# Expert slots of the lowest ranks cut from 256 to 242–254 rows, with a partial second block in a mixture-of-experts kernel

## The chip, the cores and the metric

The kernel runs on one core of a Trainium2 chip. The metric is the device time of one execution in microseconds (us); lower is better.

## What is computed

A two-block sequence model over 2048 tokens of width 1024. The first block is a retention and pooling mixer, a mixture of experts and a gated embedding; the second is latent attention beside a state-space model. The change lies in the mixture of experts:

```python
logits = xt @ router_w + router_b                    # 2048 tokens, 32 experts
top_vals, top_idx = lax.top_k(logits, 4)             # each token goes to 4 experts
gates = jax.nn.softmax(top_vals, axis=-1)
...                                                  # rows sorted by expert
gu = lax.ragged_dot(xs, w_gu, group_sizes) + b_gu    # 1024 -> 2048
gate = jnp.minimum(gu[:, ::2], 7.0)
up = jnp.clip(gu[:, 1::2], -7.0, 7.0)
act = (up + 1.0) * (gate * jax.nn.sigmoid(1.702 * gate))
y = lax.ragged_dot(act, w_down, group_sizes) + b_down   # 1024 -> 1024
out = out.at[tok].add(y * gates)                     # added back to each token's row
```

## The kernel before

**Slots.** The 32 experts are sorted on the chip by how many rows they got, and slot j takes the expert of rank j. A slot has a fixed number of rows, `CAPS[j]` (line 49): 312 for the first down to 260 for the 19th, then 256 for the last thirteen (ranks 19 to 31). An expert with fewer rows is filled up with entries of a padding row; what exceeds a slot would be done in an overflow loop of 128-row blocks, which runs zero times with these inputs, before and after.

**One slot.** `start` loads the slot's entries (`ent`: token numbers and gates) by SP, and `gather` lets POOL fetch the token rows by two indirect DMAs of 128 rows (L866, tile `rows`). `turn` transposes a block of 128 rows on PE and splits it into a high and a low part, `xTh` and `xTl`, 128 partitions by n columns, n being the slot's rows. All products are made of three (`mm3`, L142 to L144: high by high, high by low, low by high).

`gate_up` holds a 128x128 block of weights still and moves the n columns of `xTh`/`xTl` past it: 8 column groups x 2 x 8 x 3 = 384 products a slot, n columns each. `swiglu` makes `aTh`/`aTl` of the result. For a slot of 256 rows `down_rows` holds 128 columns of `aTh`/`aTl` still and moves 512 columns of weights: 2 halves h of the output width x 4 pieces x 2 row blocks b x 2 x 3 = 96 products. At the end of each half `done` adds the bias (DVE, L1081), multiplies by the gate (ACT, L1082) and issues on POOL an indirect DMA (L1083) that adds the 128 rows of `yrow`, 2 KB each, to the token rows of `x_h` in DRAM: two scatters, b = 0 and b = 1, behind each half.

**Weights.** A slot's weights come in 24 pieces of 512 KB (16 for `gate_up`, 8 for `down_rows`), one SP DMA each into `raw` (3 buffers); ACT makes `whi` (L135, L160) and DVE `wlo` (L136, L161), 3 buffers each, in the order in which the pieces are used. So a piece's load can begin only when the split three pieces earlier is done.

**Rows above 256** of larger slots go together: four slots share one gather, and after the last of them one small scatter for each slot and half (L1043, tile `rest`) adds `CAPS[j] - 256` rows. The group of ranks 2 to 5 has, in the order of issue, 40, 32, 32 and 24 rows; ranks 0 and 1 have 56 and 48.

**Order of the work.** `S.later(n, f)` queues an action n pieces ahead: the next slot's `start` one piece after the slot before began, its four `turn`s from eight pieces on. State-space work of the second block is interleaved with the slots by the same queue.

Of the kernel before, what the change touches and what calls it, by code (L numbers as in the profile page):

```python
# [15 lines left out]
F32 = mybir.dt.float32  # L16
# [4 lines left out]
OP = mybir.AluOpType  # L21
# [24 lines left out]

CAPS = [312, 304, 296, 288, 288, 280, 280, 280, 280, 272, 272, 272, 272, 264, 264, 264] + [260] * 3 + [256] * 13
NOV = 96  # L50
LE = T + 128
TR = T + 512
# [7 lines left out]
def _const_table():  # L60
    cols = []

    def put(name, a):
        a = np.asarray(a, np.float64)
        if a.ndim == 1:
            a = np.broadcast_to(a, (128, a.shape[0]))
        off = sum(c.shape[1] for c in cols)
        _CST[name] = (off, a.shape[1])
        cols.append(np.ascontiguousarray(a).astype(np.float32))
# [19 lines left out]
    col[:32, 1] = 31 - np.arange(32)  # L89
    col[:32, 2] = CAPS  # L90
    put("ecol", col)
# [41 lines left out]
def split(S, hi, lo, src):  # L133

    S.nc.scalar.activation(hi, src, AF.Copy)  # L135
    S.nc.vector.tensor_tensor(lo, src, hi.bitcast(F32), op=OP.subtract)  # L136


def mm3(S, ps, a, b, start, stop):

    nc = S.nc
    nc.tensor.matmul(ps, a[0], b[0], start=start, stop=False)  # L142
    nc.tensor.matmul(ps, a[0], b[1], start=False, stop=False)  # L143
    nc.tensor.matmul(ps, a[1], b[0], start=False, stop=stop)  # L144


def piece(S, src, shape, g=None):

    nc = S.nc
    raw = S.wp.tile([128, 1024], F32, name="raw", bufs=S.wbufs[0])  # L150
    hi = S.wp.tile([128, 1024], F32R, name="whi", bufs=S.wbufs[1])
    lo = S.wp.tile([128, 1024], F32R, name="wlo", bufs=S.wbufs[1])
    n = shape[0] * shape[1]
    r, h, w = [x[:, :n].rearrange("p (a b) -> p a b", a=shape[0]) for x in (raw, hi, lo)]
    nc.sync.dma_start(r, src)
    if g is None:
        split(S, hi[:, :n], lo[:, :n], raw[:, :n])
    else:
        for k in range(shape[0]):
            nc.scalar.activation(h[:, k, :], r[:, k, :], AF.Copy, scale=g[:, k:k + 1])  # L160
            nc.vector.scalar_tensor_tensor(w[:, k, :], r[:, k, :], g[:, k:k + 1], h[:, k, :].bitcast(F32),  # L161
                                           op0=OP.mult, op1=OP.subtract)
    return h, w
# [72 lines left out]
def transposes(S, dst, src, n):  # L236

    for i in range(n):
        S.nc.tensor.transpose(dst[:, i, :], src[:, i * 128:(i + 1) * 128], S.ident)  # L239
# [603 lines left out]
def shared():  # L843

    out = [[]]
    for j, n in enumerate(CAPS):
        if n > 256:
            if sum(CAPS[i] - 256 for i in out[-1]) + n - 256 > 128:
                out.append([])
# [30 lines left out]
def expert(S, j):  # L880
    return S.nc.sync.value_load(S.erow[0:1, j:j + 1], min_val=0, max_val=NE - 1)


def start(S, j):
    s = S.slots[j] = Slot()
    s.j, s.n = j, CAPS[j]
    s.e = expert(S, j)
    fetch(S, s, S.X["list"][ds(s.e * LE, len(blocks(s.n)) * 128)])
    s.sh = None
    for js in shared():  # L890
        if j == js[0]:
            g = S.sh = Slot()
            g.slots, g.at, g.n = js, {}, 0
            g.ent = S.xp.tile([128, 2, 2], I32, name="ent", bufs=5)
            for i in js:
                m = CAPS[i] - 256
                e = s.e if i == j else expert(S, i)
                S.nc.sync.dma_start(g.ent[g.n:g.n + m, 0], S.X["list"][ds(e * LE + 256, m)])
                g.at[i] = slice(g.n, g.n + m)
                g.n += m  # L900
            gather(S, g, 1, g.n)
        if j in js:
            s.sh, s.at = S.sh, S.sh.at[j]
            s.rest = S.xp.tile([s.n - 256, 2], I32, name="rest", bufs=12)
            S.nc.sync.dma_start(s.rest, S.X["list"][ds(s.e * LE + 256, s.n - 256)])


def phase_c(S):
    nc, A, X = S.nc, S.A, S.X
    wg = A["expert_w_gate_up"][0]  # L910
    wd = A["expert_w_down"][0]
    with ExitStack() as es:
# [33 lines left out]
        def turn(s, b, q):  # L946
            o = b * 128
            ps = S.ps.tile([128, 4, 128], F32, name="tp", bufs=2)
            transposes(S, ps, s.rows[b][:, q * 512:(q + 1) * 512], 4)
            split(S, s.xT[0][:, q * 4:q * 4 + 4, o:o + 128], s.xT[1][:, q * 4:q * 4 + 4, o:o + 128], ps)  # L950

        def turn_shared(g, q):
            n = g.n
# [7 lines left out]
        def turns(s, j):  # L961

            prepare(s, j)
            for i in range(4):
                turn(s, i // 2, i % 2)
                yield
            if s.sh:
                if j == s.sh.slots[0]:
                    for q in range(2):
                        turn_shared(s.sh, q)  # L970
                        yield
                split(S, s.xT[0][:, :, 256:], s.xT[1][:, :, 256:], s.sh.xT[:, :, s.at])
# [14 lines left out]
        def gate_up(s, e, first=()):  # L987
            w = wg[ds(e, 1)].rearrange("o (k p) f -> p (o k) f", p=128)
            s.aT = (p.tile([128, 8, s.n], F32R, name="aTh", bufs=1), p.tile([128, 8, s.n], F32R, name="aTl", bufs=1))
            ready = list(first)  # L990
            for f in range(8):
                acc = [S.ps.tile([128, 512], F32, name="acc", bufs=4) for _ in range(2)]
                for kh in range(2):
                    h, lw = ready.pop(0) if ready else weights(w[:, kh * 4:kh * 4 + 4, f * 256:(f + 1) * 256], True)
                    for g in range(2):
                        for k in range(4):
                            kk = kh * 4 + k
                            mm3(S, acc[g][:, :s.n], (h[:, k, g, :], lw[:, k, g, :]),
                                (s.xT[0][:, kk, :], s.xT[1][:, kk, :]), kk == 0, kk == 7)
                    if kh == 1:  # L1000
                        swiglu(s, f, acc)
                    S.pump()
# [68 lines left out]
        def down_rows(s, e):  # L1071

            w = wd[ds(e, 1)].rearrange("o (k p) f -> p (o k) f", p=128)
            bias = p.tile([128, D], F32, name="bd", tag="br", bufs=1)
            bsrc = A["expert_b_down"][0][ds(e, 1)]
            nc.sync.dma_start(bias, bsrc.broadcast_to([128, D]))
            adds = []

            def done(h, b, acc):
                y = p.tile([128, 512], F32, name="yrow", bufs=3)  # L1080
                nc.vector.tensor_add(y, acc, bias[:, h * 512:(h + 1) * 512])  # L1081
                nc.scalar.mul(y, y, s.ent[:, b, 1:2].bitcast(F32))  # L1082
                add = nc.gpsimd.indirect_dma_start(  # L1083
                    out=X["h1", h], out_offset=bass.IndirectOffsetOnAxis(ap=s.ent[:, b, 0:1], axis=0),
                    in_=y, in_offset=None, compute_op=OP.add)
                for a in adds:
                    S.tc.declare_no_dep(add.ins, a.ins, reason="an expert has no token twice")
                adds.append(add)

            for h in range(2):  # L1090
                acc = [S.ps.tile([128, 512], F32, name="acc", bufs=4) for _ in range(2)]
                for kp in range(4):
                    wh, wl = piece(S, w[:, kp * 2:kp * 2 + 2, h * 512:(h + 1) * 512], (2, 512))
                    for b in range(2):
                        for k in range(2):
                            kk = kp * 2 + k
                            mm3(S, acc[b], [x[:, kk, b * 128:(b + 1) * 128] for x in s.aT], (wh[:, k, :], wl[:, k, :]),
                                kk == 0, kk == 7)
                        if kp == 3:
                            done(h, b, acc[b])  # L1100
                    S.pump()
# [5 lines left out]
        slots = S.slots  # L1107
# [7 lines left out]
        with S.tc.For_i(0, n, 1) as i:  # L1115
            s = Slot()
# [24 lines left out]
        for j in range(NE):  # L1141
            if j + 1 < NE:
                S.later(1, lambda j=j: start(S, j + 1))
                S.later(8, lambda j=j: S.steps(2, turns(slots[j + 1], j + 1)))
            if j == 1:
                S.later(2, s5)
            gate_up(slots[j], slots[j].e, ready if j == 0 else ())
            (down_rows if slots[j].n == 256 else down)(slots[j], slots[j].e)
        S.drain()


# [1083 lines left out]
```

## Time and profile before

| | |
|---|---|
| time, three runs | 4979.05, 4980.39 and 4987.18 us, median 4980.39 us |
| profiled execution | 4985.11 us: a span of 4983.3 us and 1.8 us around it |
| PE busy in the span | 4882.0 us (98%) |
| the slots of 256 rows | about 2444 to 3352 us of the span, some 70 us each |
| mean granted clock of TensorE | 0.993 of full speed |

A time counts the whole execution; the span runs from the first to the last instruction of the profiled one, and all points of time below are counted from its start.

### The profile page before, as it was taken

What the parts mean: (1) busy time and instruction counts of PE and PEld (TensorE: products, weight loads), DVE (VectorE), ACT (ScalarE), POOL (GpSimd) and SP (SyncE); (2) the same over time, 40 slices, a digit from 0 to 9 for tenths busy, and PEclk for the clock granted to TensorE, in tenths of its full rate; (3) what the DMA queues carried; (4) which work ended last, traced back from release to release, by engine and by line L of the source; (5) the groups of instructions that cost most, each with busy time, mean ns of one, the idle gap of its engine ahead of it and who ended that gap; (6) DMA issues with size and microseconds to landing.
All of it is one profiled execution on the core that took longest, in us unless ns stands there. A gap on an engine that the chain in (4) does not pass through costs nothing.

```text
span 4983.3 us, 85621 instructions
## 1 busy us (share of the span) xinstructions
PE 4882.0 (98%) x31503; PEld 4420.4 (89%) x31503; DVE 3414.1 (69%) x7271; ACT 2588.7 (52%) x4530; POOL 901.7 (18%) x910
## 2 busy tenths in 40 slices
PE   9999999899999999999999999999999999999999
PEld 7888788799999999999998999987888888888877
DVE  5666565486666676776777777666666577788686
ACT  4333344455555555555555555545555466666653
POOL 2212234011121103011211111113332300000011
PEclk9999999899999999999999999999999999999999
DMA  5332365566666667676677767766554533222243
GB/s 175 97 95 86 126 234 174 165 188 189 189 202 191 209 184 216 187 222 201 207 223 225 226 212 225 215 210 193 178 175 154 164 112 93 86 71 66 76 151 102
DMA packets 620263, 834.10 MB, mean 167 GB/s; under 512 B 76116, under 2 KB 451716, under 8 KB 619808
## 3 DMA queue, kind: packets, MB, share of 16 engines
q1 hardware_dynamic: 554976, 648.34, 40.7%
q0 software_dynamic: 64864, 180.24, 13.1%
q8 instruction: 250, 4.10, 0.3%
q14 instruction: 173, 1.42, 0.1%
HBM read 685.42 MB, written 143.02 MB: 166 GB/s over the span
## 4 chain that ended last, share of the span: by engine, by line
PE 50%; DVE 5%; DMA 2%; ACT 1%; issue 1%; SPq 0%; POOL 0%; DVEq 0%; ACTq 0%; POOLq 0%
PE acc L142 12%; PE acc L143 12%; PE acc L144 12%; PE tp L239 2%; PE tp L1914 1%; PE oc L142 1%; PE oc L143 1%; PE oc L144 1%; DVE pl L136 1%; DVE mx L1969 1%; PE sc L142 1%; PE sc L143 1%; PE sc L1967 1%; PE sc L144 1%; PE sc L1968 1%
## 5 line engine op out<-in xcount | busy, mean ns | idle before, releaser
L136 DVE TENSOR_TENSOR wlo<-raw,whi 128x1024 fp32r<-128x1024 f32 x810 | 991.3, 1224 | 620.9 <-ACT whi L135 609.9
L135 ACT ACTIVATE whi<-raw 128x1024 fp32r<-128x1024 f32 x810 | 901.0, 1113 | 884.0 <-PE acc L143 440.1
L142 PE MATMUL acc<-xTh,whi 128*128 128x256 f32 (+8 forms) x4096 | 1188.0, 291 | 0.8 <-ACT whi L135 0.8
L144 PE MATMUL acc<-xTh,wlo 128*128 128x256 f32 (+8 forms) x4096 | 1172.5, 288 | 2.1 <-DVE wlo L136 2.0
L143 PE MATMUL acc<-xTl,whi 128*128 128x256 f32 (+8 forms) x4096 | 1174.0, 287 | 0.0
L142 PEld LDWEIGHTS acc<-xTh,whi 128*128 128x128 f32 x4096 | 773.8, 189 | 4.2 <-issue 2.3
L143 PEld LDWEIGHTS acc<-xTl,whi 128*128 128x128 f32 x4096 | 774.6, 189 | 1.0 <-issue 0.5
L144 PEld LDWEIGHTS acc<-xTh,wlo 128*128 128x128 f32 x4096 | 770.4, 189 | 3.3 <-DVE wlo L136 3.1
L143 PE MATMUL acc<-wlo,hTh 128*128 128x512 f32 (+1 forms) x1728 | 679.9, 394 | 0.8 <-DVE wlo L161 0.8
L142 PE MATMUL acc<-whi,hTh 128*128 128x512 f32 (+1 forms) x1728 | 674.6, 398 | 5.0 <-ACT hTh L135 4.3
L144 PE MATMUL acc<-whi,hTl 128*128 128x512 f32 (+1 forms) x1728 | 677.3, 395 | 0.0
L142 PEld LDWEIGHTS acc<-whi,hTh 128*128 128x128 f32 x1728 | 324.6, 189 | 73.1 <-ACT hTh L135 6.0
L143 PEld LDWEIGHTS acc<-wlo,hTh 128*128 128x128 f32 x1728 | 325.9, 189 | 68.0 <-DVE wlo L161 2.0
L144 PEld LDWEIGHTS acc<-whi,hTl 128*128 128x128 f32 x1728 | 325.5, 188 | 67.8 <-DVE hTl L136 0.7
L143 PE MATMUL acc<-aTl,whi 128*128 128x280 f32 (+7 forms) x1216 | 350.4, 291 | 0.2
L142 PE MATMUL acc<-aTh,whi 128*128 128x280 f32 (+7 forms) x1216 | 350.4, 295 | 0.0
L144 PE MATMUL acc<-aTh,wlo 128*128 128x280 f32 (+7 forms) x1216 | 348.7, 291 | 0.0
L142 PEld LDWEIGHTS acc<-aTh,whi 128*128 128x128 f32 x1216 | 226.8, 188 | 6.1 <-ACT whi L135 4.1
L143 PEld LDWEIGHTS acc<-aTl,whi 128*128 128x128 f32 x1216 | 229.2, 189 | 0.7 <-DVE aTl L136 0.7
L144 PEld LDWEIGHTS acc<-aTh,wlo 128*128 128x128 f32 x1216 | 227.6, 188 | 0.0
L1969 DVE TENSOR_REDUCE mx<-sc 128x1 f32<-128x512 f32 x256 | 174.8, 686 | 71.8 <-PE sc L1968 70.2
L866 POOL DMA_INDIRECT rows<-x_xm,row x68 | 81.2, 1194 | 758.3 <-PE acc L144 290.4
(618 smaller groups left out, 9726.0 us busy)
## 6 DMA issues: line engine op xcount, KB each, us to landing
raw<-expert_w_gate_up SPq DMA_DIRECT2D x512, 512.0 KB
raw<-expert_w_down SPq DMA_DIRECT2D x256, 512.0 KB
raw<-w_in SPq DMA_DIRECT2D x128, 512.0 KB
raw<-w_out SPq DMA_DIRECT2D x32, 512.0 KB
raw<-ple_gate_w SPq DMA_DIRECT2D x32, 512.0 KB
ag<-x_ag SPq DMA_DIRECT2D x16, 768.0 KB
x<-x SPq DMA_DIRECT2D x16, 512.0 KB
x_mixT<-mixst POOLq DMA_DIRECT2D x32, 256.0 KB, 4.0
```

Source lines behind the costliest of these rows:

```text
L135: S.nc.scalar.activation(hi, src, AF.Copy)
L136: S.nc.vector.tensor_tensor(lo, src, hi.bitcast(F32), op=OP.subtract)
L142: nc.tensor.matmul(ps, a[0], b[0], start=start, stop=False)
L143: nc.tensor.matmul(ps, a[0], b[1], start=False, stop=False)
L144: nc.tensor.matmul(ps, a[1], b[0], start=False, stop=stop)
L239: S.nc.tensor.transpose(dst[:, i, :], src[:, i * 128:(i + 1) * 128], S.ident)
L866: nc.gpsimd.indirect_dma_start(out=r[:n], out_offset=None, in_=X["xm"], in_offset=bass.IndirectOffsetOnAxis(ap=s.row[:n, b:b + 1], axis=0))
L1914: nc.tensor.transpose(ps[:, kk, t, :], P[t][kt // 4][:, (kt % 4) * 128:(kt % 4 + 1) * 128], S.ident)
L1967: nc.tensor.matmul(Sc[c], qh[:, tr], krT[:, cs], start=False, stop=False)
L1968: nc.tensor.matmul(Sc[c], ql[:, tr], krT[:, cs], start=False, stop=True)
L1969: nc.vector.tensor_reduce(mx[:, c:c + 1], Sc[c], axis=AX.X, op=OP.max)
```

## The change

The last eleven of the thirteen slots of 256 rows get 254, 254, 252, 250, 250, 248, 248, 246, 244, 242 and 242 rows. In all 86 rows are left out. `turn` splits only the first n − 128 columns of the second block; `gate_up` moves n columns; in `down_rows` the second block holds n − 128 columns of `aTh`/`aTl` still, and its bias, gate and scatter take n − 128 rows. The gathers still take 128 rows.

```diff
-CAPS = [312, ..., 264, 264, 264] + [260] * 3 + [256] * 13
+CAPS = [312, ..., 264, 264, 264] + [260] * 3 + [256, 256, 254, 254, 252, 250, 250, 248, 248, 246, 244, 242, 242]
...
             transposes(S, ps, s.rows[b][:, q * 512:(q + 1) * 512], 4)
-            split(S, s.xT[0][:, q * 4:q * 4 + 4, o:o + 128], s.xT[1][:, q * 4:q * 4 + 4, o:o + 128], ps)
+            m = min(s.n - o, 128)
+            split(S, s.xT[0][:, q * 4:q * 4 + 4, o:o + m], s.xT[1][:, q * 4:q * 4 + 4, o:o + m], ps[:, :, :m])
...
             def done(h, b, acc):
+                m = min(s.n - b * 128, 128)
                 y = p.tile([128, 512], F32, name="yrow", bufs=3)
-                nc.vector.tensor_add(y, acc, bias[:, h * 512:(h + 1) * 512])
-                nc.scalar.mul(y, y, s.ent[:, b, 1:2].bitcast(F32))
+                nc.vector.tensor_add(y[:m], acc[:m], bias[:m, h * 512:(h + 1) * 512])
+                nc.scalar.mul(y[:m], y[:m], s.ent[:m, b, 1:2].bitcast(F32))
                 add = nc.gpsimd.indirect_dma_start(
-                    out=X["h1", h], out_offset=bass.IndirectOffsetOnAxis(ap=s.ent[:, b, 0:1], axis=0),
-                    in_=y, in_offset=None, compute_op=OP.add)
+                    out=X["h1", h], out_offset=bass.IndirectOffsetOnAxis(ap=s.ent[:m, b, 0:1], axis=0),
+                    in_=y[:m], in_offset=None, compute_op=OP.add)
...
                         for k in range(2):
                             kk = kp * 2 + k
-                            mm3(S, acc[b], [x[:, kk, b * 128:(b + 1) * 128] for x in s.aT], (wh[:, k, :], wl[:, k, :]),
+                            mm3(S, acc[b][:min(s.n - b * 128, 128)],
+                                [x[:, kk, b * 128:min(s.n, (b + 1) * 128)] for x in s.aT], (wh[:, k, :], wl[:, k, :]),
                                 kk == 0, kk == 7)
...
-            (down_rows if slots[j].n == 256 else down)(slots[j], slots[j].e)
+            (down_rows if slots[j].n <= 256 else down)(slots[j], slots[j].e)
```

On PE, where `gate_up` of the first slot of 250 rows ends and its `down_rows` begins, the order before is this (the shape is that of the result):

```order
L143 MATMUL acc<-xTl,whi 128x256
L144 MATMUL acc<-xTh,wlo 128x256
L142 MATMUL acc<-whi,aTh 128x512
L143 MATMUL acc<-wlo,aTh 128x512
L144 MATMUL acc<-whi,aTl 128x512
L142 MATMUL acc<-whi,aTh 128x512
L143 MATMUL acc<-wlo,aTh 128x512
L144 MATMUL acc<-whi,aTl 128x512
L142 MATMUL acc<-whi,aTh 128x512
L143 MATMUL acc<-wlo,aTh 128x512
L144 MATMUL acc<-whi,aTl 128x512
```

and of the change this:

```order
L143 MATMUL acc<-xTl,whi 128x250
L144 MATMUL acc<-xTh,wlo 128x250
L142 MATMUL acc<-whi,aTh 128x512
L143 MATMUL acc<-wlo,aTh 128x512
L144 MATMUL acc<-whi,aTl 128x512
L142 MATMUL acc<-whi,aTh 128x512
L143 MATMUL acc<-wlo,aTh 128x512
L144 MATMUL acc<-whi,aTl 128x512
L142 MATMUL acc<-whi,aTh 122x512
L143 MATMUL acc<-wlo,aTh 122x512
L144 MATMUL acc<-whi,aTl 122x512
```

No product has moved or gone: those of `gate_up` are 6 columns narrower, and those of the second row block give 122 rows instead of 128. On DVE, around the ends of the two halves of the same `down_rows` (`yrow` is the block that the scatter takes, `v_L` belongs to the state-space work), the order before is this:

```order
L136 TENSOR_TENSOR wlo<-raw,whi 128x1024
L1081 TENSOR_TENSOR yrow<-acc,bd 128x512
L1675 TENSOR_SCALAR v_L_33189<-v_L_33189 128x1152
L1081 TENSOR_TENSOR yrow<-acc,bd 128x512
L136 TENSOR_TENSOR wlo<-raw,whi 128x1024 x2
L862 TENSOR_SCALAR row<-ent 128x2
L136 TENSOR_TENSOR wlo<-raw,whi 128x1024 x2
L1081 TENSOR_TENSOR yrow<-acc,bd 128x512 x2
```

and of the change this:

```order
L136 TENSOR_TENSOR wlo<-raw,whi 128x1024
L1083 TENSOR_TENSOR yrow<-acc,bd 128x512
L1678 TENSOR_SCALAR v_L_33189<-v_L_33189 128x1152
L1083 TENSOR_TENSOR yrow<-acc,bd 122x512
L136 TENSOR_TENSOR wlo<-raw,whi 128x1024 x2
L862 TENSOR_SCALAR row<-ent 128x2
L136 TENSOR_TENSOR wlo<-raw,whi 128x1024 x2
L1083 TENSOR_TENSOR yrow<-acc,bd 128x512
L1083 TENSOR_TENSOR yrow<-acc,bd 122x512
```

The second `yrow` of each half, and with it the second scatter, has 122 rows; nothing stands elsewhere. The rows of POOL, SP and ACT keep their order, and so do those of DVE and PE but for a few transposes of gathered rows and, later in the attention, of its score blocks, which stand some places earlier or later.

## Rows read from the trace of the kernel before

**Rows 1.** The page's head: the span, then busy time by engine.
```profile
span 4983.3 us, 85621 instructions
...
PE 4882.0 (98%) x31503; PEld 4420.4 (89%) x31503; DVE 3414.1 (69%) x7271; ACT 2588.7 (52%) x4530; POOL 901.7 (18%) x910
```

**Rows 2.** PE's waits, 2477 to 3354 us: total us, times, longest.
```profile
PE acc L144 <- DVE wlo L136: 1.1, 2, 0.8
```

**Rows 3.** Windows: stretch, length, busy PE PEld DVE ACT POOL, clock, DMA share, GB/s.
```profile
2790.00:3075.00 285.00, 285.00 (x2016) 263.77 (x2016) 204.44 (x303) 151.28 (x204) 44.47 (x31) 1.00 0.73 222
3286.40:3332.00 45.60, 45.60 (x386) 45.57 (x385) 34.03 (x54) 23.59 (x33) 3.75 (x2) 1.00 0.70 218
```

**Rows 4.** Windows, tile aTh alone: one whole down_rows (POOL has no column).
```profile
3122.90:3145.30 22.40, 19.92 (x64) 11.78 (x64) 0.42 (x1) 0.40 (x1) 1.00 0.71 192
```

**Rows 5.** PE's timeline: start, us, instruction; ten products lie between the first two.
```profile
1818.73 0.28 PE L143 MATMUL acc<-xTl,whi 128*128 128x272 f32 x1
...
1819.98 0.29 PE L144 MATMUL acc<-xTh,wlo 128*128 128x272 f32 x1
...
669.10 1.06 PE L634 MATMUL ret<-rw,xmT 128*128 128x32 f32 x8
669.99 0.28 PE L664 MATMUL ret<-macc,ones 128*128 128x32 f32 x1
```

**Rows 6.** POOL's timeline: second scatter of rank 29's first half, first of its second.
```profile
3209.14 1.55 POOL L1083 DMA_INDIRECT x_h<-yrow,ent  x1 [0.30 <-ACT whi L135]
...
3221.63 1.85 POOL L1083 DMA_INDIRECT x_h<-yrow,ent  x1 [7.67 <-ACT yrow L1082]
```

**Rows 7.** DMA queues (packets, MB, share) in 3207–3210, 3210–3213 (two rows), 3363–3365 us.
```profile
q1 hardware_dynamic: 893, 0.62, 70.2%
...
q0 software_dynamic: 187, 0.35, 104.5%
q1 hardware_dynamic: 94, 0.08, 9.9%
...
q0 software_dynamic: 135, 0.25, 67.0%
```

**Rows 8.** POOL's timeline: a 40-row and a 24-row scatter of ranks 2 to 5.
```profile
1440.03 1.43 POOL L1043 DMA_INDIRECT x_h<-yrow,rest  x1 [0.30 <-issue]
...
1454.51 1.40 POOL L1043 DMA_INDIRECT x_h<-yrow,rest  x1 [3.62 <-DMA x_h<-yrow,rest]
```

**Rows 9.** DMA packets, ends of 40-, 24- and 56-row scatters (1442.83, 1457.05, 1116.9 us on).
```profile
DMA packets 73, 0.07 MB, mean 97 GB/s; under 512 B 10, under 2 KB 63, under 8 KB 73
...
DMA packets 48, 0.13 MB, mean 291 GB/s; under 512 B 12, under 2 KB 12, under 8 KB 48
...
DMA packets 117, 0.16 MB, mean 121 GB/s; under 512 B 14, under 2 KB 80, under 8 KB 116
```

**Rows 10.** Chain that ended last, 3130 to 3335 us: start, us, what.
```profile
3139.68 10.10 DMA raw<-expert_w_gate_up
...
3152.34 0.39 PE acc L144
...
3213.16 9.01 DMA raw<-expert_w_gate_up
...
3224.71 6.76 DMA raw<-expert_w_gate_up
...
3234.03 0.39 PE acc L144
```

**Rows 11.** ACT's waits, 2424 to 3332 us: total us, times, longest.
```profile
ACT whi L135 <- DMA raw<-expert_w_gate_up: 88.7, 48, 6.1
```

**Rows 12.** Windows behind the last slot (columns as in Rows 3).
```profile
3352.00:3362.00 10.00, 2.43 (x11) 1.62 (x9) 4.12 (x6) 3.56 (x6) 3.11 (x2) 0.75 0.85 238
3362.00:3372.00 10.00, 8.82 (x38) 6.85 (x38) 1.48 (x3) 2.96 (x6) 3.62 (x7) 0.74 0.78 217
```

**Rows 13.** Chain behind the last slot: its last scatter, from issue to landing.
```profile
3358.54 9.05 DMA x_h<-yrow,ent
```

More of the change, by code (lines that the diff above doesn't have):

```diff
@@ L45, in _pieces @@
     return out
-CAPS = [312, 304, 296, 288, 288, 280, 280, 280, 280, 272, 272, 272, 272, 264, 264, 264] + [260] * 3 + [256] * 13
+CAPS = [312, 304, 296, 288, 288, 280, 280, 280, 280, 272, 272, 272, 272, 264, 264, 264] + [260] * 3 + [256, 256, 254, 254, 252, 250, 250, 248, 248, 246, 244, 242, 242]
 NOV = 96
```

## The prediction

> **What bounds the kernel now.** I read the page's head first: PE is busy in 98% of the span [rows 1]. That is an average, so I asked for the stretch of the change alone: from 2477 to 3354 us PE waits 1.1 us in all [rows 2], at the full clock [rows 3]. So each column that a product doesn't move there should shorten the kernel, unless something else is as late as PE. The chain of waits says that something nearly is: at the end of each slot it leaves PE and runs through loads of `expert_w_gate_up`, of 10.10 us at 3139.68, of 9.01 and 6.76 us at 3213.16 and 3224.71, and comes back to PE by way of a split, with the first product that needs it at 3152.34 and 3234.03 [rows 10]. PE doesn't wait there, and it has nothing to spare either. ACT, which makes `whi` from these loads, waits 88.7 us for them in 48 places [rows 11]. While PE is the bound over most of a slot, the loads behind a slot's scatters arrive just in time.
>
> **Why those loads are long.** They lie behind the scatters. POOL issues the second scatter of rank 29's first half at 3209.14, until 3210.69, and the first of the second half at 3221.63 [rows 6]. In 3207–3210 weight loads (q1) hold 70.2% of the 16 DMA engines; in 3210–3213, with scatters and gathers under way (q0, 104.5%), they get 9.9% [rows 7]. A piece is spread over all engines, so it lands when the slowest engine has got through its scatter rows.
>
> **Price of a product's columns.** 386 products of 256 columns stand in 45.60 us with nothing between them: 118.1 ns each [rows 3]. The 96 products of a `down_rows` move 512 columns in 22.40 us: 233.3 ns [rows 4]. That makes 0.45 ns a column. Between 256 and 272 columns it is less: ten products of 272 start within 1.25 us, 125 ns, thus 0.43 ns a column [rows 3, 5]. A floor could lie below: products of only 32 columns come every 111 ns (eight in 0.89 us) [rows 5], what a 128-column weight block costs anyway. Going down by 0.45 ns a column from 118.1, 242 columns reach 111.8 ns, just above this floor.
>
> **The gain.** The slots lose 2+2+4+6+6+8+8+10+12+14+14 = 86 rows, each a column of 384 products: 33,024 columns. At 0.43 to 0.45 ns they are 14.2 to 14.9 us. I take 14. All of it is on PE in stretches where PE is the bound. `down_rows` gives nothing: its products still move 512 columns, past a block of 114 to 126 columns in place of 128. The narrower additions, multiplications and splits of DVE and ACT have free time beside them (0.72 and 0.53 busy) [rows 3]; and the transposes that change places stand between products that are there anyway. I count both as nothing; if a moved transpose of the attention came in too late, a few tenths of a microsecond each.
>
> The Trainium skill has a lower price: its page TensorE: Matmul & The Clock Gate, section Back-to-back issue gap, gives some 81 ns for a product of 128 columns and 131 ns for 512 in a stream of weight loads and products. By that a column is 0.13 ns, and the 33,024 would be an estimated 4.3 us. The trace does not agree: 118 and 233 ns at 256 and 512 columns.
>
> **The second scatter.** 22 scatters now have 126, 126, 124, 122, 122, 120, 120, 118, 116, 114 and 114 rows, where there were 128. Fewer rows, but over how many engines? The small scatters of larger slots show it. Each engine that took part ends with a small packet (under 512 B), and at the ends of the 40-, 24- and 56-row scatters there are 10, 12 and 14 of these [rows 8, 9]. 24 and 56 would come out so by filling engines with equal whole numbers of rows, too; 40 would not: three rows each would need 14 engines. 10 is the largest number up to 16 by which 40 can be divided, 12 that for 24, 14 that for 56. By that 128 rows go to 16 engines, 8 rows each, and the new ones go
>
> - 126 to 14 engines, 9 rows each: 1 more on the busiest;
> - 124 to 4, 31 each: 23 more;
> - 122 to 2, 61 each: 53 more;
> - 120 to 15, 8 each: none;
> - 118 to 2, 59 each: 51 more;
> - 116 to 4, 29 each: 21 more;
> - 114 to 6, 19 each: 11 more.
>
> A row takes an engine 0.176 us where it is least disturbed: 67.0% of 16 engines for 2 us, by 0.25 MB in rows of 2 KB (122) [rows 7]. In 3210–3213 the same quotient is 0.29 us (104.5% x 16 x 3 us by 171), with gathers and loads in between. I take 0.176. Then a scatter holds back the load behind it by 0.2, 4.0, 9.3, 0, 9.0, 3.7 and 1.9 us; over the eleven slots (two each of 126, 122, 120 and 114) the first halves make 0.4+4.0+18.6+0+9.0+3.7+3.8 = 39.5 us, and so do the second halves.
>
> **What comes through to PE.** Behind the first half the load has nothing to spare, so I count all but some 5 us that splits and small leads absorb: 34. From it to the second half some 12.5 us pass [rows 6], in which 0.27 of the engines' time is free [rows 3], up to 3.4 us that loads regain; off seven delays of 1.9 us and more, this leaves (0.6 + 2x5.9 + 5.6 + 0.3) = 18 us; I take 16. The last scatter of all, on the chain between the slots and the next phase [rows 13], takes 1.9 of these with it. Loss: 50 us. Bounds: 25 us, if loads in flight on other pieces make up half; 79 us, if both halves come through in full, or the first halves at 0.29 us a row (65) with 16 behind them. A stall can also halve the clock: after the pause of PE at the end of the slots the granted clock is 0.75 and 0.74 in two windows of 10 us [rows 12], that is at 1.2 GHz in place of 2.4 for about half of each, 5 us of work in all. For two or three of the long stalls this adds up to 8 us at most to the upper bound; I take none.
>
> **Sum.** 4985.1 − 14 + 50 = 5021 us for the profiled execution. That execution took 4.7 us more than the median of the three runs, so I forecast 4980.4 + 36 = **5017 us**. This case's own range is 4980.4 − 14 + 25 = 4992 to 4980.4 − 14 + 79 + 8 = 5053.
>
> **Rivals.**
> - *The extra rows cost nothing* (ends on the other side). The partial scatters are dealt out evenly over 16 engines, or pieces already in the three buffers cover the delay. For it: POOL waits for nothing here, and 122 rows are less work than 128. Against it: 10 engines for 40 rows, and loads with nothing to spare. Only the gain remains: 4980.4 − 14 = 4966 us. It decides where less than 4 us of the 50 come through. The Trainium skill's page DMA: Bandwidth & Descriptors, section Why a DMA increments its semaphore by 16 and not by 1, has both: the number of engines is the largest up to 16 that divides the dimension, but on trn2 some direct copies issued by POOL go to 16 engines with the rows divided by 16 and rounded up. By this exception 122 rows would be at most 8 an engine, as 128 are; the count of 10 at 40 rows agrees with the first rule, not with the exception. Chance 0.15.
> - *Gain and loss cancel.* Delays come through at about a quarter, some 14 us, because only those of 9 us reach PE: 4976 to 4990. Chance 0.14.
> - *Products below 256 columns get no cheaper*, held at today's 118 ns by their weight loads, with scatters spread evenly: 4980 us, within the 0.2% of no change. With the uneven deal: 5031 us, inside the range. For it: the floor of 111 ns is near. Against it: the slope is still 0.43 at 256. Chance 0.08, half of it beside the uneven deal.
> - *Products below 256 columns fall into a slower way of running.* Nothing in the trace has this width in this kind; at the 233 ns of 512 columns, the nearest row above, the eleven slots would lose 384 x 11 x 0.115 = 486 us. Chance 0.03.
>
> **How the numbers follow.** The likeliest case has 0.6. Slower by over 0.2% (10 us, about what runs of this kernel can tell, three of which lie 8 us apart): the likeliest case, half of the third rival and the fourth, 0.68 with some of the second's upper edge. Faster: 0.16, the first rival and a little of the second. Same: the rest of the second, the even half of the third and weaker forms of the first, 0.16. The range runs from the first rival to the upper bound of the likeliest: 4964 to 5053; outside lie the fourth, and stalls that cost more than the bound.
>
> **What the changed profile would show.** If I am right: `gate_up` products 1 to 6 ns closer together with each slot; PE waiting in the last eleven slots, for `whi` or `wlo` behind loads, 30 us or more in all, where it waits 1.1 now; these waits sitting at the ends of the 250- and 246-row slots, 5 to 20 us each slot, some at 252 and 244, and none at 248, where the rows divide by 15; at a 122-row scatter's end 2 small packets in place of 16. The forecast is wrong if the waits stay near 1 us (even deal), if they follow the order of the slots and not the divisors, or if products of 250 columns are no closer than those of 256.

## The result, and the profile after

The changed kernel takes 5014.78 us (median of nine runs, 5001.35 to 5031.3), the kernel before 4987.06 us (median of nine): a ratio of 1.0056, with a 95% interval from 1.0047 to 1.0064. It is 28 us slower. The forecast was 37 us slower (4980.4 to 5017 us). The profiled execution has a span of 5009.1 us, 25.8 us longer than before.

PE's waits in the slots of 256 to 242 rows (total us, times, longest) are the first thing to look at; before, there was one row of 1.1 us [rows 2]:

```profile
PE acc L142 <- ACT whi L135: 13.1, 10, 2.4
PE acc L144 <- DVE wlo L136: 7.1, 10, 0.8
PE tp L239 <- DMA rows<-x_xm,row: 3.9, 1, 3.9
```

The windows of the profile after, cut just behind the scatters of each slot's first half, say where (length, busy PE, PEld, DVE, ACT and POOL, granted clock, DMA share, GB/s). The windows begin there in the slots of 254, 254, 252, 250, 250, 248, 248, 246, 244 and 242 rows and run to the same place of the next slot:

```profile
2640.00:2712.00 72.00, 70.55 (x496) 64.27 (x495) 50.44 (x77) 36.70 (x51) 10.26 (x8) 1.00 0.73 215
2712.00:2785.00 73.00, 72.47 (x509) 65.96 (x508) 56.38 (x88) 38.22 (x53) 9.35 (x7) 1.00 0.71 209
2785.00:2862.00 77.00, 73.88 (x517) 68.73 (x517) 55.55 (x78) 39.52 (x53) 13.83 (x13) 0.98 0.75 223
2862.00:2940.00 78.00, 72.77 (x498) 65.87 (x498) 49.09 (x76) 36.91 (x52) 12.40 (x7) 0.96 0.67 201
2940.00:3018.00 78.00, 74.11 (x508) 66.79 (x508) 49.99 (x77) 38.08 (x53) 11.86 (x8) 0.98 0.67 197
3018.00:3086.00 68.00, 68.00 (x497) 63.47 (x496) 48.68 (x73) 36.13 (x49) 10.62 (x7) 1.00 0.75 224
3086.00:3155.00 69.00, 68.19 (x497) 63.21 (x496) 48.33 (x73) 35.98 (x48) 9.58 (x6) 1.00 0.76 221
3155.00:3234.00 79.00, 74.37 (x500) 68.72 (x499) 49.53 (x74) 36.70 (x49) 12.58 (x7) 0.91 0.67 194
3234.00:3308.00 74.00, 70.11 (x497) 64.56 (x497) 47.98 (x72) 36.43 (x49) 10.79 (x7) 0.98 0.70 206
3308.00:3374.00 66.00, 66.00 (x481) 61.09 (x479) 45.70 (x68) 33.97 (x44) 7.92 (x5) 1.00 0.73 212
```

Length less PE's busy time is PE's idle time: 3 to 5 us behind the slots of 252, 250, 250, 246 and 244 rows, under 1.5 us behind those of 254, 248 and 242. The same five windows, and no others, have a clock below 1.00. The idle time of these windows is 23.6 us (with the 160 us ahead of them, 24.2), where the same work had about 1 before. The clock lost at most (1 − 0.98) x 77 + (1 − 0.96) x 78 + (1 − 0.98) x 78 + (1 − 0.91) x 79 + (1 − 0.98) x 74 = 14.8 us; it is less as far as PE stood still meanwhile.

The chain at the end of the first slot of 250 rows (start, us, what) runs through a load of 14.21 us, where the loads behind a first half's scatters had 9 to 10 us before [rows 10]:

```profile
2866.81 14.21 DMA raw<-expert_w_gate_up
2881.12 1.13 ACT whi L135
2882.30 0.57 PE acc L142
```

Behind the slot of 246 rows, in 3171–3173 us, the DMA view gives (first the busy tenths of the 16 engines in 40 slices, then each queue's packets, MB and share):

```profile
DMA  3422242024202509220402210224205122242054
...
q0 software_dynamic: 45, 0.10, 24.3%
q1 hardware_dynamic: 20, 0.02, 3.8%
```

Scatters hold 24.3% of the engines, as much as four of 16: by the rule of divisors two for each of the two scatters of 118 rows. The rest stand nearly idle, and the weight loads (q1) get 3.8%: 20 packets beside 45 of the scatters. One packet takes 0.243 x 16 x 2 us / 45 = 0.173 us of its engine, close to the 0.176 us of the sum.

The page's fourth part, on the chain, has 2% of the span for loads of this line and 5% for all DMA; before, all DMA had 2% (first the row of before, then two of the change):

```profile
PE 50%; DVE 5%; DMA 2%; ACT 1%; issue 1%; SPq 0%; POOL 0%; DVEq 0%; ACTq 0%; POOLq 0%
...
PE 47%; DVE 6%; DMA 5%; ACT 2%; issue 1%; SPq 0%; POOL 0%; DVEq 0%; ACTq 0%; POOLq 0%
PE acc L144 11%; PE acc L142 11%; PE acc L143 11%; DMA raw<-expert_w_gate_up 2%; PE tp L239 2%; PE tp L1917 1%; PE oc L142 1%; PE oc L144 1%; PE oc L143 1%; DVE pl L136 1%; DVE mx L1972 1%; PE sc L142 1%; PE sc L143 1%; PE sc L1971 1%; PE sc L1970 1%
```

### The profile page after: what moved, and what is told of

Same layout as the page of the kernel before. It is cut to its first block, busy times and chain, and to the rows that moved or that the text cites. A ratio compares the mean times of both kernels' runs of the same rounds, so it can differ in the third digit from the quotient of the medians.

```text
span 5009.1 us, 85623 instructions
## 1 busy us (share of the span) xinstructions
PE 4885.1 (98%) x31503; PEld 4416.4 (88%) x31503; DVE 3407.5 (68%) x7271; ACT 2585.9 (52%) x4530; POOL 910.9 (18%) x910
## 4 chain that ended last, share of the span: by engine, by line
PE 47%; DVE 6%; DMA 5%; ACT 2%; issue 1%; SPq 0%; POOL 0%; DVEq 0%; ACTq 0%; POOLq 0%
PE acc L144 11%; PE acc L142 11%; PE acc L143 11%; DMA raw<-expert_w_gate_up 2%; PE tp L239 2%; PE tp L1917 1%; PE oc L142 1%; PE oc L144 1%; PE oc L143 1%; DVE pl L136 1%; DVE mx L1972 1%; PE sc L142 1%; PE sc L143 1%; PE sc L1971 1%; PE sc L1970 1%
## 5 line engine op out<-in xcount | busy, mean ns | idle before, releaser
L142 PE MATMUL acc<-xTh,whi 128*128 128x280 f32 (+15 forms) x4096 | 1188.8, 291 | 13.7 <-ACT whi L135 13.7
L144 PE MATMUL acc<-xTh,wlo 128*128 128x280 f32 (+15 forms) x4096 | 1173.0, 288 | 8.0 <-DVE wlo L136 7.8
L143 PE MATMUL acc<-xTl,whi 128*128 128x280 f32 (+15 forms) x4096 | 1173.1, 287 | 0.0
```

## The experiments

The theory: narrower products gain; the partial second scatters are dealt to as many DMA engines as divide their rows, and the weight loads behind them wait for the busiest. Rivals: A, the narrow or odd-width products are what costs; B and D, a partial scatter costs by itself, whatever its number of rows.

**The scatters alone, and the products alone.** The first takes the kernel before and gives `done` the rows of the change:

```diff
+                m = min(ROWS[s.j] - b * 128, 128)        # 256 less 0 to 14 rows, as in the change
-                nc.vector.tensor_add(y, acc, bias[:, h * 512:(h + 1) * 512])
+                nc.vector.tensor_add(y[:m], acc[:m], bias[:m, h * 512:(h + 1) * 512])
...
-                    in_=y, in_offset=None, compute_op=OP.add)
+                    in_=y[:m], in_offset=None, compute_op=OP.add)
```

> The kernel before with one part of the change: all slots and products stay at 256 columns, and only the second yrow and scatter of each half have 126 to 114 rows in the last eleven slots (the rows left out are padding). Theory (a partial scatter goes to as many engines as divide its rows, and the weight loads wait for the busiest): the loss without the gain, 28 us of the changed kernel plus the 14 us that the narrower products give, so 42 us slower than before (30 to 55), with pauses of PE behind the slots of 252, 250, 246 and 244 rows and none behind those of 248. Rival A (the narrower products or operands of odd pitch are what costs): no change, within 5 us of before.

Measured: 5021.6 against 4987.57 us, 34 us slower (ratio 1.0067, 1.0054 to 1.0081). The other keeps the change but for the second block of `down_rows`:

```diff
+            s.na = 256 if 128 < s.n < 256 else s.n
+            s.aT = (p.tile([128, 8, s.na], ...), p.tile([128, 8, s.na], ...))
+            for x in s.aT:
+                if s.na > s.n:
+                    nc.vector.memset(x[:, :, s.n:].bitcast(F32), 0.0)
...
             def done(h, b, acc):
-                m = min(s.n - b * 128, 128)
+                m = 128
```

> The changed kernel with its narrower turns and gate_up, but aTh and aTl 256 columns wide, the columns from n on filled with zeros (two fills on DVE a slot), so that products of down_rows, yrow and scatters have 128 rows again. Theory: the gain without the loss, 14 us faster than before (10 to 16), PE waiting about 1 us in the last eleven slots as in the kernel before. Rival A: 28 us slower than before, as the changed kernel. If products below 256 columns get no cheaper: the time of before.

Measured: 4976.66 against 4987.57 us, 11 us faster (ratio 0.9981, 0.9972 to 0.9990). So the loss sits in the partial scatters and the gain in the products, and rival A falls: the narrow products are there and the kernel is faster. The gain is 3 us less than forecast, which the interval (5 to 14 us) just allows. PE's waits in the last slots:

```profile
PE acc L144 <- DVE wlo L136: 4.6, 9, 0.8
```

I had expected about 1 us, as before. DVE has two fills more in each of these slots; whether they make the difference I did not test.

**One size in all eleven slots.** Each of these four kernels is the changed one with another list:

```diff
-... [256, 256, 254, 254, 252, 250, 250, 248, 248, 246, 244, 242, 242]
+... [256] * 2 + [248] * 11        # or 250, 252, 254
```

> The changed kernel with 248 rows in each of the last eleven slots (88 rows fewer than before in all, the changed kernel has 86 fewer). Second scatters of 120 rows: 15 engines with 8 rows each by the theory, no engine busier than with 128 rows. Theory: 14 us faster than before (10 to 16). Rival B (any scatter that doesn't take all 128 partitions costs, on whatever number of engines; the measured 42 us are 3.8 us a slot): 27 us slower than before.

> The changed kernel with 250 rows in each of the last eleven slots (66 rows fewer than before). Second scatters of 122 rows: 2 engines with 61 rows each by the theory. The two slots of this size in the changed kernel pushed the work behind them back by some 8.5 and 6.5 us. Theory: eleven times 7.5 us less 11 us of gain, 71 us slower than before (50 to 110). Rival B: 3.8 us a slot less 11 us, 31 us slower than before; rival A the same order as the changed kernel, 28 us slower.

> The changed kernel with 252 rows in each of the last eleven slots. Second scatters of 124 rows: 4 engines with 31 rows each by the theory of divisors. The one slot of this size in the changed kernel pushed the work behind it back by some 5 us net of the gain in columns. Theory: 11 x 5.5 us of loss less 384 x 11 x 1.5 ns = 6 us of gain, 54 us slower than before (25 to 65), between 248 (9 us faster) and 250 (90 us slower). Rival B (a loss that grows with the rows left out): between 254 and 250 in a straight line.

> The changed kernel with 254 rows in each of the last eleven slots. Second scatters of 126 rows: 14 engines with 9 rows each by the theory of divisors, one row more than with 128. Theory: a loss of 11 x 0.2 us or less, and no gain, since products of 254 columns come every 118.5 ns where 256 take 118.3: within 4 us of before. Rival B (every partial scatter costs some 8 us a slot, as in 250): 80 us slower than before.

| rows of a slot | second scatter, by the rule | against before | ratio (95%) | packets under 512 B beyond those of before |
|---|---|---|---|---|
| 254 | 126 = 14 engines x 9 | +1.7 us | 1.0002 (0.9993 to 1.0011) | 397 |
| 252 | 124 = 4 x 31 | +50.1 us | 1.0106 (1.0091 to 1.0121) | 8184 |
| 250 | 122 = 2 x 61 | +89.8 us | 1.0179 (1.0165 to 1.0193) | 18788 |
| 248 | 120 = 15 x 8 | −9.0 us | 0.9983 (0.9974 to 0.9992) | 176 |

The loss rises, then disappears with two rows fewer. That is no line in the rows left out, and no price of partial scatters as such; it follows the divisors. Rival B falls. The sizes fit less well than the order: 250 cost 19 us more than I had expected, and 248 gained 5 us less (its interval, 4 to 14 us, still holds the 14).

The last column settles the deal without any time. It comes from the packets that each run's page counts (before, the four kernels in the table's order, the change):

```profile
DMA packets 620263, 834.10 MB, mean 167 GB/s; under 512 B 76116, under 2 KB 451716, under 8 KB 619808
...
DMA packets 620616, 834.01 MB, mean 167 GB/s; under 512 B 76513, under 2 KB 452113, under 8 KB 620161
...
DMA packets 628359, 833.98 MB, mean 166 GB/s; under 512 B 84300, under 2 KB 459900, under 8 KB 627904
...
DMA packets 638919, 833.98 MB, mean 164 GB/s; under 512 B 94904, under 2 KB 470504, under 8 KB 638464
...
DMA packets 620263, 833.74 MB, mean 167 GB/s; under 512 B 76292, under 2 KB 451892, under 8 KB 619808
...
DMA packets 627463, 833.80 MB, mean 166 GB/s; under 512 B 83488, under 2 KB 459088, under 8 KB 627008
```

Suppose that k engines take r rows each, and that each of the other 16 − k gets a small packet where these get a row. Then 22 scatters of one size add 22 x (16 − k) x r small packets: by the rule 396, 8184, 18788 and 176, as counted but for a single one. In the changed kernel the rule gives 4 x 18 + 2 x 372 + 4 x 854 + 4 x 8 + 2 x 826 + 2 x 348 + 4 x 190 = 7372 for its sizes from 126 down to 114, and 7372 are counted. An even deal of 122 rows over 16 engines, eight at most, would add 132. The views do not name the engines, so where the small packets go is a reading of their number.

In the kernel of 250 rows the DMA view shows what the deal does to the loads. In 3223.8–3224.9 us, after the scatters of one slot, the DMA view is (as above):

```profile
DMA  1120211211211211211211202112112112112112
...
q1 hardware_dynamic: 52, 0.05, 13.7%
q0 software_dynamic: 1, 0.00, 0.1%
```

13.7% of 16 is 2.2 engines: while some two of them still carry their share of a weight piece, the others have nothing to do. The chain of this slot has two loads behind scatters, 3 to 5 us longer than the 9.01 (or 10.10) and 6.76 us of before [rows 10]:

```profile
3196.06 13.33 DMA raw<-expert_w_gate_up
...
3211.90 12.18 DMA raw<-expert_w_gate_up
```

**The same rows, dealt evenly.** The changed kernel with two scatters in place of each partial one; the 18 to 30 entries from row 96 on come into a tile of their own by one SP DMA a slot:

```diff
+    if s.n < 256:
+        s.tail = S.xp.tile([s.n - 224, 2], I32, name="rest", bufs=12)
+        S.nc.sync.dma_start(s.tail, S.X["list"][ds(s.e * LE + 224, s.n - 224)])
...
+                for ids, o, e in [(s.ent[:, b, 0:1], 0, 128)] if m == 128 else [(s.ent[:96, b, 0:1], 0, 96), (s.tail[:, 0:1], 96, m)]:
                     add = nc.gpsimd.indirect_dma_start(
-                    in_=y[:m], in_offset=None, compute_op=OP.add)
+                        in_=y[o:e], in_offset=None, compute_op=OP.add)
```

> The changed kernel with the same rows, but each partial second block goes out in two scatters, of its first 96 rows and of the other 18 to 30 (whose entries SP loads once more into a tile of their own). By the rule of divisors 96 rows take 16 engines with 6 each, and 18 to 30 rows take 9 to 15 engines with 2 each: nowhere more than 8. POOL issues a third scatter in each half. Theory (the uneven deal is the cost): 8 to 11 us faster than before, PE waiting no more than some 5 us in the last eleven slots. Rival D (a partial scatter costs by itself, or by POOL's longer issue, 2.9 us where 128 rows take 1.6 to 1.9): at least as slow as the changed kernel, 28 us slower than before.

Measured: 4973.37 against 4986.03 us, 13 us faster (ratio 0.9972, 0.9961 to 0.9983); the view of PE's waits has no row of the last slots. Products, additions and rows are those of the changed kernel. The dealing differs, with a scatter more in each half and a small load more in each slot, and the 28 us of loss are gone. Rival D falls: partial scatters, and more of POOL's time for them, are still there.

**One half at a time.** The scatter-only kernel with 122 rows in the eleven slots, in one of the two halves:

```diff
-                m = min(ROWS[s.j] - b * 128, 128)
+                m = 122 if s.j > 20 and b == 1 and h == 0 else 128     # or h == 1
```

> The kernel before with all products at 256 columns and 122-row second scatters in the first halves (h = 0) of the last eleven slots alone; the second halves keep 128 rows. With 250 rows in all eleven slots the loss without the gain was some 90 + 5 = 95 us. By the split of the prediction (first halves 34, second halves 16 of 50, since loads regain some lead in between): 65 us slower than before. Rival E (the two halves count alike): 47 us. Rival F (a lone delay is absorbed, and only the two together reach PE): under 20 us.

> As the run of the first halves, with the 122-row scatters in the second halves (h = 1) of the last eleven slots alone. By the split of the prediction: 30 us slower than before. Rival E: 47 us. Rival F: under 20 us.

Measured: first halves 5065.31 against 4986.03 us, 79 us slower (ratio 1.0158, 1.0144 to 1.0172); second halves 5056.63, 71 us slower (1.0136, 1.0121 to 1.0152). All my expectations failed here. Each half costs nearly as much alone as both together, some 95 us (89.8 measured, and an estimated 5 of gain in that kernel). In the chain of the run with first halves, one load behind a scatter takes

```profile
3195.06 15.78 DMA raw<-expert_w_gate_up
```

and in that of the second halves 15.81 us (at 3199.46). So what one half causes largely covers what the other would cause. The four busy engines in 3171–3173 us above point to a way: both scatters of a slot, issued 11 us apart, are under way there at once, so their delays need not add. That this is the whole reason is not shown.

**Widths in multiples of 4.** The traces up to here showed products of 254 columns no closer than those of 256. Two kernels start from the one with 128-row second blocks. In the first only the list differs:

```diff
+... [256] * 3 + [252] * 3 + [248] * 4 + [244, 240, 240]
```

> The kernel of full_scatter (128-row second blocks, columns from n on filled with zeros) with slots in multiples of 4: 256, 256, 256, 252, 252, 252, 248, 248, 248, 248, 244, 240, 240 (88 rows fewer than before; the changed kernel has 86 fewer). In the traces so far products of 256, 252, 248 and 244 columns come every 118.3, 116.8, 114.7 and 113.4 ns, those of 254, 250 and 242 every 118.5, 117.3 and 113.8. Theory (a width that is no multiple of 4 costs about 1 ns a product): 384 x (3 x 1.5 + 4 x 3.6 + 4.9 + 2 x 6.6) ns = 14 us faster than before, 3 us faster than full_scatter. Rival (the spacing is set by the count of columns alone and the differences are chance): 11 us faster, as full_scatter.

Measured: 4975.44 against 4985.85 us, 10 us faster (0.9981, 0.9972 to 0.9990). In the second the list is the change's and the tiles are wider:

```diff
+            na = max(s.n, 256)
+            s.xT = [p.tile([128, 8, na], F32R, name=x, bufs=2)[:, :, :s.n] for x in ("xTh", "xTl")]
```

> The kernel of full_scatter with the same widths as the changed kernel, but xTh and xTl laid out 256 columns apart, so that every row of them begins at a multiple of 16 bytes; n columns of them are used. Theory P (the pitch of the moving operand is what costs 1 ns at 254, 250 and 242): products of 254 and 250 come every 117.4 and 115.7 ns, and the kernel is 14 us faster than before. Rival Q (the width itself costs, wherever the rows begin): 118.5 and 117.3 ns as now, 11 us faster than before.

Measured: 4975.38 us, 10 us faster (0.9980, 0.9971 to 0.9989). Neither time can be told from the 11 us of the same kernel without the edit. The spacing in the traces (from one product's start to the next one's) says more. Windows of the last `gate_up`, all its products in a row, for the kernel with 254 in all slots, for the one with 242 (128-row second blocks), and for 240 (from the last run below):

```profile
3288.04:3333.68 45.64, 45.64 (x385) 45.63 (x384) 33.47 (x54) 23.80 (x32) 3.79 (x2) 1.00 0.71 217
```

```profile
3280.08:3323.86 43.78, 43.78 (x386) 43.77 (x384) 32.96 (x55) 23.56 (x32) 3.74 (x2) 1.00 0.73 225
```

```profile
3271.33:3314.44 43.11, 43.11 (x386) 43.10 (x385) 32.82 (x53) 23.27 (x32) 5.51 (x3) 1.00 0.74 224
```

A product takes 118.5, 113.4 and 111.7 ns, beside 118.1 at 256 [rows 3]. Two columns fewer, from 242 to 240, save 1.7 ns; two fewer from 256 to 254 save nothing. With 256-column pitch the products of 254 came some 0.7 ns closer, those of 250 0.5 ns farther apart: the pitch is not the cause. Nor do multiples of 4 sort the widths: 246 columns come every 114.1 ns, between the 114.7 of 248 and the 113.4 of 244. What the cause is stays open.

**The best version.** Both findings together, even dealing and multiples of 4:

```diff
-CAPS = ... [256, 256, 254, 254, 252, 250, 250, 248, 248, 246, 244, 242, 242]
+CAPS = ... [256] * 3 + [252] * 3 + [248] * 4 + [244, 240, 240]     # and the two scatters of 96 and 16 to 28 rows
```

> The two versions that did best put together: the second blocks in two scatters (96 rows and the other 16 to 28), and slots in multiples of 4 rows: 256, 256, 256, 252, 252, 252, 248, 248, 248, 248, 244, 240, 240 (88 rows fewer than before). Theory: the 14 us that the spacing of these products gives (384 x (3 x 1.5 + 4 x 3.6 + 4.9 + 2 x 6.1) ns), nothing lost: 14 us faster than before, at most 3 us faster than with the changed kernel's widths, which the measurement will hardly tell. Rival (the spacing at other widths does not count): 12 us faster.

Measured: 4966.79 against 4986.6 us, 20 us faster (ratio 0.9963, 0.9949 to 0.9977), faster than both kernels. The 14 us lie inside the interval's 11 to 25 us; that the widths count is not shown by this time alone.

## Why the prediction was right, and where not

**Slower, through the loads behind the second scatters: right.** Scatters alone are 34 us slower, and the same rows dealt evenly are 13 us faster. The deal is the one that the text gave for every size, and it sorts the slots: those of 252, 250, 246 and 244 rows stall PE, and the pair of 248, which has fewer rows than the 250s, does not.

**The gain: somewhat mis-sized.** "I take 14", by 0.43 to 0.45 ns a column; the products alone gave 11 us. The time by itself leaves room for 14, the spacing does not. In the trace of that kernel products of 254, 252, 250, 248, 246, 244 and 242 columns come every 118.6, 116.8, 117.3, 114.7, 114.1, 113.4 and 113.8 ns, those of 256 every 118.3; over the eleven slots this makes 10.8 us. The step that failed is that one slope holds at every width: from 256 to 242 columns a product became 4.7 ns cheaper in the windows above, 0.34 ns a column, and 254 gave nothing. The floor of 111 ns was not the reason: 242 columns come every 113.4 ns, still above it. (Between the two rows of 272 columns in [rows 5] stand nine products, not ten; the 125 ns count ten spacings and hold.) The estimate of 4.3 us that the prediction worked out from the Trainium skill's page TensorE: Matmul & The Clock Gate, section Back-to-back issue gap, lies below the interval of 5 to 14 us, and the trace does not agree with it.

**The loss: mis-sized, and made otherwise.** Of the 50 us that I took, some 39 came (28 and 11; the scatters alone cost 34). In the profile 23.6 us are PE's idle time, and up to 14.8 us are the clock, which I had taken as nothing and had named only for the upper bound. So two errors partly cancelled, which is luck: about half of the delay that I took came through, and the longer stalls of PE cost clock as well. That 5017 stands so near 5014.78 is luck too: the kernel before took 6.7 us more beside the change than the 4980.4 that the forecast starts from (and its terms make 5016.4). In the first 250-row slot PE stood still for 3.9 us from 2876.6 us on. In the 10 us around that pause the granted clock was 0.66, between its levels of 2.4 and 1.2 GHz, and the products behind it came every 0.21 us at first, every 0.12 us from 2885.4 on:

```profile
2876.00:2886.00 10.00, 5.81 (x30) 5.24 (x31) 3.14 (x5) 2.62 (x4) 0.00 (x0) 0.66 0.52 133
...
2880.52 1.51 PE L239 MATMUL tp<-ident,rows 128*128 128x128 f32 x6 [3.91 <-DMA rows<-x_xm,row]
...
2883.09 0.21 PE acc L144
...
2885.63 0.12 PE acc L144
```

**The signs: the slots right, the sizes not.** I had named waits of 30 us or more in all, 5 to 20 us in each slot of 250 and 246 rows. There were 24 us, and these three slots had 5.2, 3.9 and 4.6, hardly more than the 3.1 and 3.9 of 252 and 244 rows, for which the sum has less than half the delay. The first slot of 242 rows, 1.9 us a scatter in the sum, left PE no idle time. So idle time does not grow in proportion to the delay of the busiest engine. With the clock the slot of 246 rows lost most: 4.6 and up to 7.1 us. And a scatter of 122 rows does not show fewer small packets, as I had expected (2 in place of 16 at its end), but 854 more (18788 over 22).

**"First halves 34, second halves 16": wrong.** With 122 rows in all slots either half alone costs 79 or 71 us, and both 95. The step behind it, that lead is regained between the halves and the delays then add, does not describe what happens; the two costs do not add.

**A wait that I had not named.** PE waited 3.9 us for gathered rows (`rows`), once. The gathers are issued behind the partial scatter and land late too; I had looked only at weights. It comes back in the kernel of 250 rows, twice, 8.0 us in all.

**The rival on the other side** (even dealing, 4966 us) is what split scatters made true, 13 us faster where it said 14. The doubt was whether scatters on POOL's queue follow the rule of the largest divisor in the Trainium skill's page DMA: Bandwidth & Descriptors, section Why a DMA increments its semaphore by 16 and not by 1, or its exception for direct copies. For these scatters the runs of 254 to 248 rows agree with the rule, by their times (+1.7, +50.1, +89.8, −9.0 us) and by their packets, not with the exception.

## What to carry to other kernels

A scatter with fewer rows can take longer: count how many of the 16 DMA engines its row count allows before cutting rows, since a load that is spread over all engines waits for the busiest. If a remainder is needed, send it as two scatters whose row counts divide well, or leave the scatter at its full 128 rows with padding: 13 and 11 us faster than before, which the intervals do not tell apart. And when a kernel is bound by one engine at 98%, look at the chain of waits at the seams all the same: a load that arrives just in time is a second bound, and here the stalls behind it cost clock too.

## What the runs showed of the hardware

- A scatter-add on POOL's queue was dealt to the largest number of engines up to 16 that divides its rows, at each size from 114 to 126 rows: the counts of small packets fit but for one packet (the sizes of 114 to 118 rows only in the sum of 7372).
- A scatter that adds 2 KB rows keeps an engine 0.17 to 0.18 us a row. While two of them ran, the weight loads got 3.8% of the engines, and at the end of a piece some 14 engines had nothing left to do.
- POOL's own time for issuing a scatter grows with the rows of its busiest engine (9, 31 and 61 by the rule). Second scatters in three kernels, of 126, 124 and 122 rows:

```profile
3072.38 1.58 POOL L1085 DMA_INDIRECT x_h<-yrow,ent  x1 [0.30 <-ACT whi L135]
```

```profile
3169.10 2.21 POOL L1085 DMA_INDIRECT x_h<-yrow,ent  x1 [0.30 <-ACT whi L135]
```

```profile
3192.06 2.94 POOL L1085 DMA_INDIRECT x_h<-yrow,ent  x1 [0.30 <-ACT whi L135]
```

  These are among the shortest of each size. Others of the same size took up to 1 us longer (1.55 to 2.56 us with 128 rows), so a single issue does not tell its deal.

- A product that streams 254 columns is no cheaper than one of 256 (118.5 and 118.1 ns), one of 240 costs 111.7 ns.
